# Score products over 128 rows instead of 128 and then 64, with keys padded by zeros

## The chip, the cores and the metric

The kernel runs on one core of one Trainium2 chip. The metric is the device time of one execution in microseconds (us). Three executions of the kernel before took 2716.71 us in the median (2715.36 to 2717.19).

## The reference

The reference is a network of three blocks on 512 tokens of width 1024, with a second stream of 256 context tokens in the last two. All is in 32-bit floats. The part that matters here is attention: four kinds of it, each of heads of 64 features.

```python
# first block: three dilated bands, joined over one row of weights
logits = jnp.einsum('bhrnqd,bhrnkd->bhrnqk', qb, kb) * Dh ** -0.5 + bias[None, :, None, None]
p = jnp.exp(logits - m[..., None])
num = jnp.einsum('bhrnqk,bhrnkd->bhrnqd', p, vb)
```

The second block has a differential attention (4 heads, each the difference of two maps of 64 features, over all 768 keys for the 512 tokens and over the 256 context keys for the context) and a neighbourhood attention (8 heads, blocks of 128 queries that see 256 keys around them and the 256 context keys). The third has a grouped attention (8 query heads, 2 key heads, 512 queries by 768 keys). All else in the network (a gated delta rule beside the dilated attention, projections, feed-forward layers, a long convolution) is not touched.

## The kernel before, in words

**Split products.** Each product of 32-bit operands is made of products of two rounded parts: a = hi + lo, both in the format that TensorE takes at full rate. A projection takes three matmuls (hi hi, hi lo, lo hi, lines 323 to 325), a score two, as follows.

**Scores.** A tile of 128 rows holds the features of two heads, 64 rows each. Since one head fills only half of the 128 rows of TensorE's array, the other half carries the small parts. `stacked` (line 1544) makes from keys [128, n] a tile [128, 2, n]: in `[:, e]` the 64 rows of head e hold its high parts and the other 64 rows its low parts. It takes one copy on ACT (line 1548) and two subtractions on POOL over 64 rows (line 1550). `doubled` (line 1553) makes from 128 queries the high parts of head e on both halves of the rows, and, in `lo`, the low parts of both heads, each on its own rows (ACT line 1557, POOL lines 1558 and 1560). `scores` (line 1563) then issues two matmuls for each up to 512 keys (line 1571): the first over 128 rows, q hi times k hi plus q hi times k lo; the second over the 64 rows of head e only, q lo times k hi, added in PSUM. In the grouped attention the roles are turned: the queries are stacked, and the keys, which stand twice in the rows, are split into `kl` and `kh` by `halves`; its second matmul also takes 64 rows.

**Stages.** The work on an item (a tile of 128 queries and a head, or both maps in the differential attention) is a list of steps, load, score, turn (transpose the weights, line 435, and copy them out of PSUM, lines 1581 and 1583), apply (times the values), end. `skewing` (line 1524) lets step i of an item come with step i - 1 of the next; a load stands two steps ahead of its score. Between score and turn `exp_rows` (line 892) takes the row maximum on DVE (line 903, or 899 with a bias) and the exponential on ACT (line 904 or 901). The scores have two PSUM rooms.

- The dilated attention of the first block (`dilated`, line 910) runs beside the recurrence of the delta rule, some of its steps with every round of it. Its keys are stacked in a room of the raw weights (`wraw`).
- In the second block `diff_attention` (line 1713) and `neighbourhood` (line 1586) are one list of items. Their keys are stacked in a tile `ks` with two rooms, once for each of four heads (pairs of maps) and of four pairs of heads. The value products are on line 1758 (over 128 columns), and on lines 1643 and 1702 (over 64 columns).
- In the third block `pair_attention` (line 1669) does the grouped attention, 32 items. Its value products are on line 1702 (64 columns).

**Rooms for weights.** `wchunk` (line 306) loads 512 KB of weights into one of two raw rooms, copies the high parts to one of three rooms `whi` on ACT (line 311), and subtracts the low parts into one of three rooms `wlo` on POOL (line 312). The last projection ahead of the attention in the second block is that of `vb`; the next weights after it are those of the out-projection.

**Order.** The instructions of each engine run in the order in which a planner has put them when the program is built (`schedule_with_timeline_sim=True`). It keeps what depends on what, and otherwise takes the work in the program's order as soon as its own estimate of times says it can start; later weights are split ahead of earlier attention where rooms are free.

## Time and profile before

| | |
|---|---|
| median of three timed executions | 2716.71 us |
| the profiled execution, its span from the first to the last instruction | 2708.6 us |
| TensorE (PE) busy | 2582.3 us, 95% |
| TensorE's weight loads (PEld) busy | 2093.1 us, 77% |
| VectorE (DVE) busy | 1636.8 us, 60% |
| GpSimd (POOL) busy | 1187.8 us, 44% |
| ScalarE (ACT) busy | 981.1 us, 36% |
| chain that ended last, by engine | PE 76%, DVE 15%, DMA 3%, issue 2% |
| mean granted clock of TensorE | 0.972 |

For the profiled execution the trace gives the span; the timed executions, which start and end outside of it, are 6.8 to 8.6 us longer. Busy shares are over the whole span. Matmuls are pipelined: a new one starts before the one ahead has ended, so the spacing from start to start says what one costs in a stream, and the duration does not. The chain of waits follows the work back from the last instruction to what released it; its shares say where time would be won if a piece became shorter and nothing else came in its place.

### The profile page before, as it was taken

To read this page: it belongs to the slowest core of one execution; us is meant where nothing else is said; L and a number is where in the kernel's file an instruction comes from. 1 tells how busy PE (TensorE), PEld (TensorE's weight loads), DVE (VectorE), ACT (ScalarE), POOL (GpSimd) and SP (SyncE) were. 2 spreads that over 40 slices of the span, in tenths; PEclk is the share of its full clock that TensorE was granted. 3 is DMA by queue.
4 is the path that set the end of the run, shared out by engine and by line. 5 is a ranking of instruction groups with operands and counts; after the bars stand their busy time and mean duration, and the time that the engine had idled before them with its cause. 6 is when DMAs were issued, how large, how long until landed. Compare 5 with 4: busy or idle time off the path is not lost.

```text
span 2708.6 us, 35291 instructions
## 1 busy us (share of the span) xinstructions
PE 2582.3 (95%) x13312; PEld 2093.1 (77%) x13312; DVE 1636.8 (60%) x2896; ACT 981.1 (36%) x1727; POOL 1187.8 (44%) x827
## 2 busy tenths in 40 slices
PE   8878999999999978999999999999999999999999
PEld 6667776788888757666788888888878778788887
DVE  6987546634434798776547677767576445634333
ACT  4514434322224323375524222122244543333232
POOL 3346525555556434676514232323245215444443
PEclk9989989999999989898999999999999999999999
DMA  5251112232333244301022343424242003233333
GB/s 198 81 182 46 31 55 94 86 100 88 99 102 124 98 155 139 110 17 28 28 102 86 111 134 111 138 93 149 76 136 75 20 24 124 87 95 96 104 95 94
DMA packets 103453, 257.94 MB, mean 95 GB/s; under 512 B 11745, under 2 KB 20065, under 8 KB 102900
## 3 DMA queue, kind: packets, MB, share of 16 engines
q1 hardware_dynamic: 102708, 254.64, 29.2%
q8 instruction: 105, 1.72, 0.3%
q10 hardware_dynamic: 576, 1.05, 0.1%
q14 instruction: 64, 0.52, 0.1%
HBM read 246.06 MB, written 14.83 MB: 96 GB/s over the span
## 4 chain that ended last, share of the span: by engine, by line
PE 76%; DVE 15%; DMA 3%; issue 2%; POOL 1%; ACT 1%; SPq 0%; POOLq 0%; DVEq 0%; ACTq 0%
PE ps_mm L323 13%; PE ps_mm L325 13%; PE ps_mm L324 13%; PE ps_s L1571 5%; PE ps_mx L324 3%; PE ps_mx L325 3%; PE ps_mx L323 3%; PE ps_m L324 3%; PE ps_m L323 3%; PE ps_m L325 3%; PE ps_t L435 3%; DVE ada_j L1093 2%; PE ps_pv L1702 2%; DVE ada_w L1093 2%; DMA ada_w<-in_w_ada 2%
## 5 line engine op out<-in xcount | busy, mean ns | idle before, releaser
L312 POOL TENSOR_TENSOR wlo<-wraw,whi 128x1024 fp32r<-128x1024 f32 (+2 forms) x344 | 776.3, 2260 | 1116.5 <-ACT whi L311 1034.8
L311 ACT ACTIVATE whi<-wraw 128x1024 fp32r<-128x1024 f32 (+2 forms) x345 | 336.8, 978 | 968.4 <-PE ps_mm L324 479.1
L323 PE MATMUL ps_mm<-h,whi 128*128 128x512 f32 (+1 forms) x1496 | 540.7, 363 | 11.8 <-ACT whi L311 7.3
L325 PE MATMUL ps_mm<-h,wlo 128*128 128x512 f32 (+1 forms) x1496 | 539.5, 362 | 2.3 <-POOL wlo L312 2.3
L324 PE MATMUL ps_mm<-h,whi 128*128 128x512 f32 (+1 forms) x1496 | 539.4, 362 | 1.2 <-DVE h L1145 1.0
L323 PEld LDWEIGHTS ps_mm<-h,whi 128*128 128x128 f32 x1496 | 282.4, 189 | 57.1 <-ACT whi L311 7.3
L325 PEld LDWEIGHTS ps_mm<-h,wlo 128*128 128x128 f32 x1496 | 282.0, 189 | 48.9 <-POOL wlo L312 2.9
L324 PEld LDWEIGHTS ps_mm<-h,whi 128*128 128x128 f32 x1496 | 282.2, 189 | 47.4 <-issue 1.7
L1093 DVE CUSTOM_DVE_ANT_0 ada_j<-ada_w,ada_c 128x512 f32<-128x512 f32 x192 | 195.9, 1020 | 14.7 <-DMA ada_w<-in_w_ada 14.2
L1093 DVE CUSTOM_DVE_ANT_0 ada_w<-ada_w,ada_c 128x512 f32<-128x512 f32 x192 | 186.2, 970 | 4.0
L325 PE MATMUL ps_mm<-fa,wlo 128*128 128x512 f32 (+1 forms) x528 | 186.3, 356 | 1.4 <-POOL wlo L312 1.4
L324 PE MATMUL ps_mm<-fa,whi 128*128 128x512 f32 (+1 forms) x528 | 187.6, 356 | 0.0
L323 PE MATMUL ps_mm<-fa,whi 128*128 128x512 f32 (+1 forms) x528 | 185.7, 356 | 0.0
L1270 DVE SCALAR_TENSOR_TENSOR cb<-ps_mm,small,cb 128x511 f32<-128x511 f32 (+1 forms) x66 | 43.6, 660 | 188.8 <-ACT cb L1268 188.8
L1218 DVE SCALAR_TENSOR_TENSOR x<-ps_mm,mod,x 128x512 f32<-128x512 f32 x80 | 59.4, 748 | 138.4 <-PE ps_mm L325 131.4
L903 DVE TENSOR_REDUCE nm<-ps_s 128x1 f32<-128x768 f32 (+1 forms) x96 | 74.6, 777 | 63.6 <-PE ps_s L1571 63.0
L325 PEld LDWEIGHTS ps_mm<-fa,wlo 128*128 128x128 f32 x528 | 99.0, 188 | 18.0 <-POOL wlo L312 2.0
L324 PEld LDWEIGHTS ps_mm<-fa,whi 128*128 128x128 f32 x528 | 99.2, 188 | 16.0
L323 PEld LDWEIGHTS ps_mm<-fa,whi 128*128 128x128 f32 x528 | 98.9, 188 | 16.4 <-ACT whi L311 0.3
L324 PE MATMUL ps_mx<-h,whi 128*128 128x512 f32 x216 | 86.1, 399 | 3.0 <-DVE h L1005 3.0
L323 PE MATMUL ps_mx<-h,whi 128*128 128x512 f32 x216 | 85.8, 399 | 0.5 <-ACT whi L311 0.5
L325 PE MATMUL ps_mx<-h,wlo 128*128 128x512 f32 x216 | 85.7, 397 | 0.0
(490 smaller groups left out, 5234.5 us busy)
## 6 DMA issues: line engine op xcount, KB each, us to landing
ada_w<-in_w_ada SPq DMA_DIRECT2D x192, 256.0 KB
wraw<-in_w_up SPq DMA_DIRECT2D x88, 512.0 KB
wraw<-in_w_d SPq DMA_DIRECT2D x48, 384.0 KB
wraw<-in_w_d SPq DMA_DIRECT2D x53, 320.0 KB
wraw<-in_we_in SPq DMA_DIRECT2D x24, 512.0 KB
wraw<-in_w_g SPq DMA_DIRECT2D x22, 512.0 KB
wraw<-in_w_u SPq DMA_DIRECT2D x22, 512.0 KB
wraw<-in_we_out SPq DMA_DIRECT2D x13, 512.0 KB
```

Of the source, the lines that this page charges most:

```text
L311: self.S.activation(hi[:, :n], raw[:, :n], AF.Copy)
L312: (eng or self.G).tensor_tensor(out=lo[:, :n], in0=raw[:, :n], in1=hi.bitcast(F32)[:, :n], op=ALU.subtract)
L323: mm(ps, lhi, rhi, start=start, stop=False)
L324: mm(ps, lhi, rlo, start=False, stop=False)
L325: mm(ps, llo, rhi, start=False, stop=stop)
L435: last = self.PE.transpose(ps[:, j * P:(j + 1) * P], src[:, j * P:(j + 1) * P], self.ident)
L903: V.tensor_reduce(out=m, in_=src, op=ALU.max, axis=AX.X, negate=True)
L1093: V.tensor_tensor_reduce(out=(junk, w)[s], in0=w, in1=c[:, s, i * T:i * T + T], scale=0.5, scalar=0.0, op0=ALU.mult, op1=ALU.add, accum_ou ...
L1218: V.scalar_tensor_tensor(out=xs[s][:, m], in0=p[:, :w], scalar=mod[:, gate * 8 + m, s:s + 1], in1=xs[s][:, m], op0=ALU.mult, op1=ALU.add)
L1270: V.scalar_tensor_tensor(out=cb[:, t0 + 1:t1], in0=pg[s][:, :w_ - 1], scalar=fw[0], in1=cb[:, t0 + 1:t1], op0=ALU.mult, op1=ALU.add)
L1571: self.PE.matmul(p[:, c0:min(n, c0 + 512)], q[i], k[i][:, c], start=i == 0, stop=i == 1)
L1702: PE.matmul(st["v"][hs, t * P:(t + 1) * P], vals(e, kt), st["t", t, e][:, kt * P:(kt + 1) * P], start=kt == 0, stop=kt == nk - 1)
```

## The change

The second matmul of a score takes all 128 rows as well. Its query operand is `lo` as it stands, with the low parts of both heads. Its key operand is a new tile `kz`: in `[:, e]` the 64 rows of head e hold its high parts, and the other rows are zero. Two such tiles are set to zero once on POOL at the start of the dilated attention (512 columns) and of the attention of the second block (768 columns), and the own rows are filled for each pair of heads by two copies of 64 rows on ACT. In the second block they take the place of the two rooms of `ks`; the stacked keys of the two heads go to a room of `whi` and a room of `wlo`, and so the copy over both becomes one for each. In the dilated attention they stay in the raw room, also with a copy for each. In the grouped attention no tile is added: the second matmul takes the stacked queries and the low parts of the keys on all 128 rows, which adds the product of the low parts. (The diff also takes comments and descriptions out of the file.)

```diff
+    def zeroed(self, pool, n, nm="kz"):
+        tiles = [pool.tile([P, 2, n], F32R, name=f"{nm}{i}", bufs=1) for i in range(2)]
+        for z in tiles:
+            for e, (own, other) in enumerate(HALVES):
+                self.G.memset(z.bitcast(F32)[other, e], 0.0)
+        return tiles
-    def stacked(self, at, src, nm, bufs=2, st=None):
-        if st is None:
-            st = at.tile([P, 2, src.shape[-1]], F32R, name=nm + "s", bufs=bufs)
-        self.S.activation(st, self.midb(src, 2), AF.Copy)
+    def stacked(self, at, src, nm, bufs=2, kz=None, st=None):
+        n = src.shape[-1]
+        if kz is None:
+            room = at.tile([P, 2, n], F32R, name=nm + "s", bufs=bufs)
+            st = [room[:, e] for e in range(2)]
+            self.S.activation(room, self.midb(src, 2), AF.Copy)
+        else:
+            st = st or [self.wh.tile([P, CH], F32R, name=w)[:, :n] for w in ("whi", "wlo")]
+            for a in st:
+                self.S.activation(a, src, AF.Copy)
         for e, (own, other) in enumerate(HALVES):
-            self.G.tensor_tensor(out=st[other, e], in0=src[own], in1=st.bitcast(F32)[own, e], op=ALU.subtract)
-        return st
+            self.G.tensor_tensor(out=st[e][other], in0=src[own], in1=st[e].bitcast(F32)[own], op=ALU.subtract)
+        if kz is None:
+            return st
+        for e, (own, other) in enumerate(HALVES):
+            self.S.activation(kz[own, e], src[own], AF.Copy)
+        return st, [kz[:, e] for e in range(2)]
...
+        kzs = self.zeroed(da, T)
...
-                                st["k", pair] = self.stacked(da, self.dk[:, pair], "k",
-                                                       st=room.rearrange("p (e t) -> p e t", e=2))
+                                st["k", pair] = self.stacked(da, self.dk[:, pair], "k", kz=kzs[pair % 2],
+                                                             st=[room[:, :T], room[:, T:]])
...
-                        (q, lo), k = st["q", pair, qt], st["k", pair]
-                        self.scores(p[:, :n], (q[:, e], lo[hs]), (k[:, e, :n], k[hs, e, :n]))
+                        (q, lo), (k, kz) = st["q", pair, qt], st["k", pair]
+                        self.scores(p[:, :n], (q[:, e], lo), (k[e][:, :n], kz[e][:, :n]))
...
+                kzs = self.zeroed(at, TC)
...
-                            st["k", pair] = self.stacked(at, ka[:, pair], "k")
+                            st["k", pair] = self.stacked(at, ka[:, pair], "k", kz=kzs[pair % 2])
...
-                        q = q[:, e], lo[hs]
-                        k = st["k", pair][:, e], st["k", pair][hs, e]
+                        q = q[:, e], lo
+                        k = [a[e] for a in st["k", pair]]
...
-                    q = (q[:, e], q[hs, e]) if form == "stacked" else (q[0][:, e], q[1][hs])
+                    q = (q[e], q[e]) if form == "stacked" else (q[0][:, e], q[1])
...
-                        st["k", hd] = self.stacked(at, qkb[hd // 2][:, 1, hd % 2], "k")
+                        st["k", hd] = self.stacked(at, qkb[hd // 2][:, 1, hd % 2], "k", kz=kzs[hd % 2])
...
-                        (q, lo), k, hs = st["q", hd, t], st["k", hd], HALVES[e][0]
-                        self.scores(p, (q[:, e], lo[hs]), (k[:, e, k0:], k[hs, e, k0:]))
+                        (q, lo), (k, kz) = st["q", hd, t], st["k", hd]
+                        self.scores(p, (q[:, e], lo), (k[e][:, k0:], kz[e][:, k0:]))
...
-                            return self.kd2[0], self.kd2[1][HALVES[e][0]]
+                            return self.kd2
```

## Rows read from the trace of the kernel before

**Rows 1.** Stretches: length, busy us (and count) of PE, PEld, DVE, ACT, POOL, clock, DMA.
```profile
205.00:380.00 175.00, 166.39 (x1299) 134.50 (x1298) 105.27 (x268) 82.81 (x185) 96.30 (x122) 0.98 0.11 32
1137.00:1257.00 120.00, 111.72 (x507) 76.56 (x505) 81.87 (x204) 80.56 (x218) 82.59 (x112) 0.87 0.09 25
1257.00:1371.00 114.00, 110.59 (x722) 82.22 (x723) 68.55 (x189) 56.97 (x158) 56.87 (x92) 0.97 0.14 44
2106.00:2235.00 129.00, 129.00 (x769) 91.79 (x768) 55.46 (x108) 62.82 (x121) 26.02 (x38) 1.00 0.05 17
```

**Rows 2.** Chain of waits, shares by line: 205:380, 1137:1257, 1257:1371, 2106:2235.
```profile
by line: PE ps_p L760 11.4%; PE ps_p L754 11.4%; PE ps_pv L954 10.8%; PE ps_p L435 10.8%; PE ps_a L1571 8.1%; PE ps_a L435 6.3%; DVE ada_j L1093 6.0%; DVE ada_w L1093 4.3%; PE ps_a L431 2.5%; PE ps_p L720 2.5%; PE ps_p L776 2.4%; PE ps_o L8
...
by line: PE ps_s L1571 43.4%; PE ps_pv L1758 22.2%; PE ps_t L435 12.0%; POOL E L1747 3.9%; issue 3.8%; DVE nm L903 2.8%; POOL E L1748 1.9%; ACT E L904 1.8%; DVE E L1743 1.3%; DVE er L1741 1.2%; POOL ql L1558 1.1%; ACT PT L1581 0.9%; DVE PT 
...
by line: PE ps_s L1571 39.2%; PE ps_pv L1643 25.9%; PE ps_t L435 20.5%; PE ps_t L431 4.4%; PE ps_pv L1702 4.0%; PE ps_pv L1758 1.3%; DVE da_o L1768 0.9%; DVE da_o L1769 0.8%; DVE nm L903 0.7%; DVE h L319 0.6%; ACT h L318 0.5%; DVE rsq_a L30
...
by line: PE ps_s L1571 33.1%; PE ps_pv L1702 31.7%; PE ps_t L435 20.8%; PE ps_t L323 3.1%; PE ps_t L324 2.8%; PE ps_t L325 2.8%; PE ps_t L431 2.2%; PE ps_mm L323 1.2%; PE ps_mm L324 1.2%; PE ps_mm L325 1.2%
```

**Rows 3.** Timeline of PE, grouped attention: start us, us, engine, line, operation, tiles, rows*columns, shape.
```profile
2136.22 0.48 PE L1571 MATMUL ps_s<-kh,qs 128*128 128x512 f32 x1
2136.63 0.49 PE L1571 MATMUL ps_s<-kl,qs 64*128 64x512 f32 x1
2137.05 0.38 PE L1571 MATMUL ps_s<-kh,qs 128*128 128x256 f32 x1
...
2137.68 0.50 PE L1571 MATMUL ps_s<-kh,qs 128*128 128x512 f32 x1
...
2141.99 0.47 PE L1571 MATMUL ps_s<-kh,qs 128*128 128x512 f32 x1
```

**Rows 4.** Timeline of PEld, a plain stream and the grouped attention; idle before in brackets.
```profile
601.68 0.19 PEld L324 LDWEIGHTS ps_mx<-h,whi 128*128 128x128 f32 x1
...
2136.63 0.18 PEld L1571 LDWEIGHTS ps_s<-kl,qs 64*128 64x128 f32 x1 [0.24 <-issue]
```

**Rows 5.** Timeline of PE, plain streams of 512 and of 256 columns.
```profile
599.63 0.39 PE L323 MATMUL ps_mx<-h,whi 128*128 128x512 f32 x1
...
601.90 0.39 PE L324 MATMUL ps_mx<-h,whi 128*128 128x512 f32 x1
...
1599.16 0.28 PE L323 MATMUL ps_mm<-fa,whi 128*128 128x256 f32 x1
...
1599.96 0.28 PE L324 MATMUL ps_mm<-fa,whi 128*128 128x256 f32 x1
```

**Rows 6.** Timeline of PE, grouped attention: the last score matmul and the value products.
```profile
2138.86 0.38 PE L1571 MATMUL ps_s<-kl,qs 64*128 64x256 f32 x1
2139.17 1.09 PE L1702 MATMUL ps_pv<-PT,gv 128*64 128x128 f32 x8
```

**Rows 7.** Timeline of DVE and ACT, grouped attention: row maximum and exponential.
```profile
2137.78 0.96 DVE L903 TENSOR_REDUCE nm<-ps_s 128x1 f32<-128x768 f32 x1 [0.85 <-PE ps_s L1571]
...
2138.78 0.90 ACT L904 ACTIVATE E<-ps_s,nm 128x768 f32<-128x768 f32 x1 [0.52 <-DVE nm L903]
```

**Rows 8.** Copies and splits by line: duration ns min/median/max, first and last start, forms.
```profile
L1548 ACT ACTIVATE ks<-qkb x4: 1472/1478/1487, 1114.2 to 1190.0; 128x1536 fp32r<-128x1536 f32 x4
...
L1422 ACT ACTIVATE qkb<-ps_t x12: 582/598/602, 1042.8 to 1112.7; 128x512 f32<-128x512 f32 x12
...
L311 ACT ACTIVATE whi<-wraw x345: 257/1060/1140, 6.2 to 2695.0; 128x1024 fp32r<-128x1024 f32 x121, 128x640 fp32r<-128x640 f32 x27, 128x768 fp32r<-128x768 f32 x24, 128x64 fp32r<-128x64 f32 x1
L312 POOL TENSOR_TENSOR wlo<-wraw,whi x344: 318/2394/3714, 14.6 to 2695.8; 128x1024 fp32r<-128x1024 f32 x122, 128x640 fp32r<-128x640 f32 x26, 128x768 fp32r<-128x768 f32 x24
```

**Rows 9.** Groups of POOL by line: busy us, mean ns, idle before.
```profile
L678 POOL MEMSET Pw<- 128x512 f32 x2 | 1.0, 540 | 10.8 <-DVE ada_p L1093 10.8
```

**Rows 10.** A weight chunk's copy on ACT; line 1571 in the second block, first and last.
```profile
1129.50 1.06 ACT L311 ACTIVATE whi<-wraw 128x1024 fp32r<-128x1024 f32 x1 [7.23 <-PE ps_m L325]
...
L1571 PE MATMUL ps_s<-ks,qd x160: 355/385/775, 1137.5 to 1365.1; 128*128 128x256 f32 x128, 128*128 128x512 f32 x32
```

More of the change, by code (lines that the diff above doesn't have):

```diff
@@ L1492, in even_mixer @@
                 at = self.pool(ats, "at", 2, "right")
+                kzs = self.zeroed(at, TC)
+                consts += kzs,
                 values = lambda half: em.tile([P, 2, 2, TC], F32, name=f"vw{half}", tag=f"qkb{half}")
-                self.skewed(self.diff_attention(at, ps, qkb, vb, lam, oms)
+                self.skewed(self.diff_attention(at, ps, qkb, vb, lam, oms, kzs)
                             + self.neighbourhood(consts, values, at, ps, qa, ka, vc, vad, oms))
@@ L1587, in neighbourhood @@
         V, S, G, PE, Q, A = self.V, self.S, self.G, self.PE, self.Q, self.A
-        mask, biases = consts
+        mask, biases, kzs = consts
         nb = len(biases)
@@ L1623, in score @@
                             st["r", pair] = at.tile([P, 4, 2], F32, name="rr")
-                        hs = slice(64 * e, 64 * e + 64)
                         p = self.s_bank(ps)
                         q, lo = st["q", pair, b]
-                        q = q[:, e], lo[hs]
-                        k = st["k", pair][:, e], st["k", pair][hs, e]
+                        q = q[:, e], lo
+                        k = [a[e] for a in st["k", pair]]
                         win = [a[:, 0:T].rearrange("p (r c) -> p r c", c=64)[:, :, w0s[b]:w0s[b] + 32] for a in k]
@@ L1653, in neighbourhood @@
                 at, ps, qa[:, pair, T:TC], "doubled",
-                lambda e, pair=pair: (st["k", pair][:, e, T:], st["k", pair][HALVES[e][0], e, T:]), 2, 2,
+                lambda e, pair=pair: [a[e][:, T:] for a in st["k", pair]], 2, 2,
                 lambda e, kt, pair=pair: vc[:, kt, (2 * pair + e) * 64:(2 * pair + e) * 64 + 64], oms[1][:, :, pair, :])
@@ L1684, in load, with score @@
                     st["q", t] = getattr(self, form)(at, qT[:, t * P:(t + 1) * P], "q", 3)
-                def score(t=t, e=e, hs=hs):
+                def score(t=t, e=e):
                     if t == 0 and e == 0:
@@ L1711, in pair_attention, with diff_attention @@
         return items
-    def diff_attention(self, at, ps, qkb, vb, lam, oms):
+    def diff_attention(self, at, ps, qkb, vb, lam, oms, kzs):
         V, S, G, PE, Q, A = self.V, self.S, self.G, self.PE, self.Q, self.A
```

## The prediction

> **What bounds the kernel now.** I read the page's table of engines first: TensorE is busy for nearly the whole span and no other engine comes near it. A busy TensorE says little here, since the ends of matmuls are modelled, so I went on to the stages in which line 1571, the score matmul, runs. The table by stretches [rows 1] shows four of them: the dilated attention beside the recurrence (205 to 380 us), the differential attention (1137 to 1257), the neighbourhood attention (1257 to 1371) and the grouped attention (2106 to 2235). The reader is to see that the other engines stand at half to two thirds of a stretch, and that only the differential stretch has three engines above 80 of 120 us. Then the chain of waits, cut to the same stretches [rows 2]: the largest part of the chain in three of them is line 1571, with 43.4%, 39.2% and 33.1%; beside the recurrence it has 8.1%. In time that is 0.434 x 120 = 52.1, 0.392 x 114 = 44.7, 0.331 x 129 = 42.7 and 0.081 x 175 = 14.2 us, 154 us in all. That is the time the change can work on.
>
> What this time is made of is seen in the timeline of TensorE [rows 3]. A score product of 768 keys is four matmuls: 512 columns over 128 rows, 512 over 64, 256 over 128, 256 over 64. From start to start the first takes 0.41 us, the second 0.42, the two of 256 together 0.63, so 0.315 each. A plain stream that stays at 128 rows does the same columns far faster [rows 5]: ten spacings of 512 columns in 2.27 us, 0.227 each, and seven of 256 in 0.80, 0.114 each. The columns are the same, all at the full granted clock; the rest, about 0.19 to 0.2 us, is paid at each change between 128 and 64 rows. The weight loads show it too [rows 4]: in the plain stream the load (601.68) runs under the matmul ahead of its own (601.90, [rows 5]), while at the change the load starts only with its own matmul and TensorE's loader has idled 0.24 us ahead of it.
>
> **The change part by part.**
> *The second matmul over 128 rows.* No matmul is added or taken away and no column. The changes 128 to 64 within a product go, and 64 to 128 behind it, unless a value product on 64 columns comes next: there the spacing is also 0.31 [rows 6], and that change of shape remains. Two items of the grouped stage have 2.95 us of scores (2136.22 to 2139.17, [rows 3, 6]); without changes it is 2 x (2 x 0.227 + 2 x 0.114) = 1.36, plus 0.2 for the one that remains: 1.57, saving 1.38 or 47%. Two neighbourhood items have eight of 256, 8 x 0.315 = 2.52, and then 0.91 to 1.11: I take 56%. The differential stage mixes both sizes and part of it is at the lower clock (0.87 on the mean, [rows 1]), where the columns themselves take longer: 50%. For the dilated one with its sizes from 128 to 512 I take 45%. On the chain that is at most 20 + 25 + 26 + 6 = 77 us. The other end is nothing, if what is late next is right behind.
>
> *What is late next.* Grouped stage: the weights of an item need its row maximum and the exponential. From the end of the scores (2137.68) they are there at 2138.78 + 0.90 = 2139.68 [rows 7], 2.0 us later. Today TensorE covers that with the next item's scores and a value product. After the change the first item's scores end at 0.68, its weights are ready at about 2.7, and TensorE has done the other scores and the eight value products (1.09, [rows 6]) at about 2.4: it waits 0.3 us. Two items go from 5.77 (2136.22 to 2141.99, [rows 3]) to 5.77 - 1.38 + 0.3 = 4.7; sixteen such pairs give 17 us, and I take 16 for the edges. The neighbourhood stage has more slack (DVE 69, ACT 57, POOL 57 of 114 us, [rows 1]) but the same kind of chain: two thirds of 25, 17. In the differential stage DVE, ACT and POOL have 82, 81 and 83 us of 120; with all 26 us gone, 94, they would have to be busy nearly 90% while waiting for each other at every item. I take 11, with ends 26 and 0. Beside the recurrence, whose chain is mostly its own products, 2 of the 6.
>
> *The split of the keys.* Per pair of heads ACT did one copy of 128x1536 in 1.48 us [rows 8]. Now it does two of 128x768 and two of 64x768. No row has this size; between 0.60 for 512 columns and 1.06 for 1024 I put 0.83, an estimate. Four are 3.3, so 1.84 more for each of eight pairs, 14.7 us, and in the dilated stage, by 4 x 0.60 - 1.06, 1.34 for each of four, 5.4: 20 us of ACT in all. POOL's two subtractions stay. I put the 20 us at nothing on the path in the neighbourhood and the dilated stage, since ACT has 57 and 92 us free there [rows 1] and a pair is loaded two steps ahead; the differential stage's 7.4 is part of why I take only 11. If the cover is gone it is the whole 20, since exponentials queue behind the copies on ACT and TensorE waits for them. In the grouped stage nothing is added.
>
> *The zeros.* Four POOL memsets in either stage. 128x512 took 0.54 [rows 9]; by that, 2.2 us in the dilated stage and, scaled to 768 columns, 3.2 in the even layer. The latter lie ahead of 1137, when the last projection still has TensorE: nothing. The former may stand in the recurrence's way: 0 to 2.2, in the 2 us above.
>
> *The room for split weights.* The stacked keys now take turns with the weight chunks in three rooms. The first pairs wait for the last projection's chunks: a weight chunk's copy that took such a room waited until 1129.50 [rows 10]. The second pair can thus have its copies at about 1130, and POOL's subtractions have 7 us behind them until scores begin at 1137.5: nothing. At the end, the third chunk of the out-projection gets its room only behind the last scores (1365, [rows 10]) and then needs 1.06 on ACT and 2.39 on POOL [rows 8]; transposes, value products and the end of the heads still run then. 0 to 3.5 us; I take 0, as its products come third.
>
> **Sum.** 16 + 17 + 11 + 2 = 46 us off the profiled execution's span, 2708.6 to 2663. The timed runs lie around it with a median of 2716.71, 8.1 above the span; I keep that distance: 2671 us. Taken by itself this forecast has 2655 to 2687.
>
> **Rivals.**
> *The other engines take it back (2695).* If the chains of maximum, exponential and transpose close up sooner, half the gain stays: 8 + 9 + 4 + 1 = 22. For it: DVE, ACT and POOL in the differential stage. Against: the other two have room.
> *All of it (2640).* The 77 us come out whole. For it: the chain in the grouped stage has TensorE nearly alone [rows 2], and the order of instructions is planned anew. Against: the 2.0 us from scores to weights.
> *Slower: ACT's copies on the path (2717 to 2737, say 2727).* Place: ACT's queue at each load of a pair, 3.3 us in one piece in front of the exponentials, with two score banks. Price: 20 us. It decides once the drains give back under 20 us; half of that given back is plus 10. For it: in the differential stretch ACT has 81 of 120 us. Against: it waits for the scores there, and far more time lies on line 1571 than 20 us.
> *The change of rows is not what costs (2716).* If the load of weights can't run under a matmul on the same rows, a product costs load plus stream: 0.19 + 0.227 = 0.41 for 512 columns, as now, and 0.30 for 256, as now within 0.02. Nothing is won, and the copies cost little. The plain stream speaks against it: the load of 0.19 at 601.68 is over before its matmul starts at 601.90, and lies wholly under the matmul ahead, on the same 128 rows [rows 4, 5].
> This is the rule of the Trainium skill's page "TensorE: Matmul & The Clock Gate" (Part 3, The mechanism): a weight load overlaps with running matmuls only when it goes to another row group. By it the old mix of 64 and 128 rows would be no worse than the new form and the time would stay at 2716; by the rows the spacing falls to 0.227. Here the rows decide.
>
> **How the numbers follow.** The forecast has 0.52, the half gain 0.22, the whole gain 0.12, slower 0.08, no effect 0.06. A measurement of this kernel can tell about 0.2% (5.4 us) from no change. So faster 0.86, same 0.06, slower 0.08. The range goes from 2640, where the whole gain ends, to 2702, which takes in the half gain and some loss at the seams (the end of the attention, a new order of work); outside are the slower case, the case without effect and a little on either side.
>
> **What would show it.** Right: score matmuls of 512 columns about 0.23 apart and those of 256 about 0.115, but 0.31 still ahead of value products; the weight loads of the second matmuls under the first; the grouped stretch down from 129 to about 113 us, the neighbourhood from 114 to 97, the differential from 120 to about 109; longer waits of TensorE for ACT and DVE. Wrong: spacings unchanged (no effect of rows); spacings short but stretches as long as before, with TensorE waiting for the exponential behind four key copies in a row (the slower rival); stretches shorter but a new wait of the out-projection for its third chunk.

## The result: 2652.9 us, a ratio of 0.977

The changed kernel took 2652.91 us in the median of four executions (2645.98 to 2653.69), the kernel before 2716.95 on the same chip (2715.36 to 2719.39): a ratio of 0.9767, with a 95% interval of 0.9749 to 0.9785, or 64 us less. The forecast was 2671, 46 us less, with a range of 2640 to 2702; the time lies inside the range, but 2 us below the 2655 to 2687 that the forecast had claimed for itself, and nearer to the rival of 2640. The profiled executions are 57.5 us apart in span (2708.6 and 2651.1): the one lies 8.4 us below its median, the other 1.8, so 6.5 of the 64 us are not in the stages below. The changed kernel's profiled execution took 2.0 us more than its own span (2653.09 and 2651.1), so most of the 8.4, which had been read as time outside of the span, means that the profiled execution of the kernel before was a quick one.

The stages of all kernels of this study, worked out from the traces as the time between two landmarks. Behind the stroke stands how much of the stage had TensorE at the lower granted clock, 1.2 GHz. Each row is a single profiled execution.

| us / of it at 1.2 GHz | start | dilated | block 1 | projection | differential | neighbourhood | feed-forward | projection 3 | grouped | rest |
|---|---|---|---|---|---|---|---|---|---|---|
| before | 204.1/27 | 204.1/23 | 566.8/35 | 162.5/17 | 126.0/31 | 111.2/7 | 657.9/0 | 78.3/0 | 132.6/0 | 460.5/10 |
| the change | 201.2/17 | 199.1/19 | 567.0/36 | 162.4/24 | 118.7/31 | 88.9/7 | 660.0/3 | 78.3/0 | 111.0/0 | 459.6/7 |
| e1, grouped only | 203.2/24 | 203.2/16 | 564.6/28 | 162.5/24 | 127.7/34 | 111.3/7 | 661.1/3 | 78.3/0 | 111.3/0 | 459.4/7 |
| e2, second block only | 203.8/23 | 203.9/23 | 566.9/36 | 163.2/21 | 114.0/14 | 89.3/7 | 660.1/3 | 78.3/0 | 132.6/0 | 460.7/10 |
| e3, dilated only | 203.5/24 | 202.3/33 | 567.3/36 | 162.5/17 | 143.0/68 | 109.3/3 | 659.5/3 | 78.2/0 | 132.6/0 | 460.6/10 |
| e12, e3 with fillers | 204.4/26 | 195.9/18 | 565.2/31 | 160.5/21 | 145.4/34 | 109.0/7 | 660.0/7 | 78.2/0 | 132.6/0 | 460.3/10 |
| e4, same rows together | 203.5/27 | 203.3/16 | 564.6/28 | 162.3/21 | 113.0/24 | 111.7/7 | 659.2/0 | 78.3/0 | 120.8/0 | 459.5/7 |
| e5, copies twice | 199.7/21 | 210.7/53 | 567.1/35 | 162.6/24 | 115.8/21 | 88.0/7 | 660.7/7 | 78.2/0 | 111.1/0 | 460.9/10 |
| e7, no POOL in the difference | 203.2/24 | 202.4/33 | 567.2/36 | 160.6/21 | 109.3/17 | 88.2/7 | 659.0/3 | 78.2/0 | 111.3/0 | 460.7/10 |
| e8, values on 128 columns | 202.9/24 | 202.5/32 | 567.4/36 | 162.7/17 | 114.5/17 | 89.3/7 | 662.6/10 | 78.3/0 | 105.8/3 | 460.8/10 |
| e9, fillers | 200.1/21 | 200.5/23 | 564.3/32 | 162.8/17 | 114.3/14 | 88.7/7 | 657.1/0 | 78.3/0 | 111.5/0 | 460.5/10 |
| e10, e7 and e8 | 203.4/27 | 198.5/22 | 564.7/26 | 160.4/14 | 109.1/17 | 88.2/7 | 659.1/3 | 78.3/0 | 101.9/0 | 460.3/10 |
| e11, e10 and fillers | 203.4/24 | 197.7/18 | 565.0/26 | 162.7/17 | 105.7/0 | 89.4/7 | 658.6/3 | 78.2/0 | 107.0/3 | 459.8/10 |

(Landmarks, each the start of a matmul: a late projection product ahead of the dilated attention; the first out-projection product of block 1 behind it; a late product of the second block's norm; the first score; the last value product of the differential attention; the first out-projection product; a late feed-forward product; the first grouped score; the first product of the long convolution; the last product.)

Between before and the change the dilated stage has 5.0 us less, the differential 7.3, the neighbourhood 22.3, the grouped 21.6, together 56.2 of the 57.8 in the table. How far a stage moves without any edit can be read from the differential column: the changed kernel, e2 and e8 have the same order of instructions there on TensorE, VectorE, ScalarE and GpSimd, and took 118.7, 114.0 and 114.5 us, with 31, 14 and 17 us at 1.2 GHz. A microsecond at the lower clock cost some 0.3 us in this order, in which TensorE also waits for other engines.

The first view to look at is the timeline of TensorE in the grouped attention, which answers to [rows 3] and [rows 6].

```profile
2101.92 0.48 PE L1593 MATMUL ps_s<-kh,qs 128*128 128x512 f32 x1
2102.24 0.39 PE L1593 MATMUL ps_s<-kl,qs 128*128 128x512 f32 x1
2102.47 0.28 PE L1593 MATMUL ps_s<-kh,qs 128*128 128x256 f32 x1
2102.59 0.28 PE L1593 MATMUL ps_s<-kl,qs 128*128 128x256 f32 x1
2102.71 0.38 PE L435 MATMUL ps_t<-ident,E 128*128 128x128 f32 x2
2103.02 1.52 PE L1723 MATMUL ps_pv<-PT,gv 128*64 128x128 f32 x12
...
2104.88 0.48 PE L1593 MATMUL ps_s<-kh,qs 128*128 128x512 f32 x1
...
2108.81 0.28 PE L1593 MATMUL ps_s<-kl,qs 128*128 128x256 f32 x1
2109.02 1.09 PE L1723 MATMUL ps_pv<-PT,gv 128*64 128x128 f32 x8
2110.04 0.44 PE L435 MATMUL ps_t<-ident,E 128*128 128x128 f32 x2
```

From start to start the four score matmuls take 0.32, 0.23, 0.12 and 0.12 us, 0.79 in all, where they took 1.46. Only the first, behind a transpose, is longer than in a plain stream. Where value products on 64 columns come next (2108.81 to 2109.02), the last one takes 0.21, not the 0.31 of [rows 6].

The weight loads answer to [rows 4]. The load of the second matmul starts at 2102.01 and its matmul at 2102.24, so it lies under the matmul ahead.

```profile
2102.01 0.19 PEld L1593 LDWEIGHTS ps_s<-kl,qs 128*128 128x128 f32 x1
```

The table by stretches of the changed kernel, as in [rows 1], with the four stages' own bounds: dilated, differential, neighbourhood, grouped.

```profile
201.00:400.00 199.00, 181.69 (x1416) 148.25 (x1414) 119.81 (x311) 88.00 (x197) 99.69 (x123) 0.95 0.16 47
1130.00:1248.00 118.00, 90.54 (x543) 78.64 (x542) 92.08 (x217) 91.76 (x246) 91.95 (x122) 0.87 0.08 21
1248.00:1337.00 89.00, 82.10 (x715) 70.86 (x714) 63.37 (x178) 57.41 (x156) 52.22 (x84) 0.96 0.15 47
2076.00:2187.00 111.00, 110.89 (x817) 91.94 (x816) 54.33 (x109) 61.99 (x122) 20.98 (x30) 1.00 0.06 20
```

And the chain of waits in the last three of them, as in [rows 2].

```profile
by line: PE ps_pv L1779 11.8%; PE ps_s L1593 11.7%; POOL E L1768 10.4%; PE ps_t L435 7.9%; issue 7.8%; DVE E L1764 6.2%; POOL E L1769 6.0%; DVE nm L903 5.7%; DVE er L1762 5.0%; POOL qd L1582 4.3%; ACT E L904 3.0%; POOL ql L1580 3.0%; DVE rs
...
by line: PE ps_pv L1664 30.3%; PE ps_t L435 24.1%; PE ps_s L1593 19.9%; PE ps_pv L1723 6.6%; PE ps_t L431 6.3%; DVE rsq_i L301 2.2%; issue 1.2%; DVE da_o L1790 1.1%; DVE da_o L1789 1.1%; DVE PT L1605 0.8%; DVE h L319 0.8%; DVE nm L903 0.7%;
...
by line: PE ps_pv L1723 41.7%; PE ps_t L435 23.5%; PE ps_s L1593 19.2%; PE ps_t L323 3.5%; PE ps_t L431 3.4%; PE ps_t L324 3.3%; PE ps_t L325 3.1%; ACT whi L311 1.0%; ACT PT L1603 0.5%; ACT hy_x L1984 0.5%; PE ps_mm L323 0.4%; issue 0.2%; A
```

The reader is to see two things. In the neighbourhood and the grouped stage TensorE still has nearly the whole chain, and is busy for 82 of 89 and 111 of 111 us: nothing has come in the place of the score matmuls, and they fell from 39.2% and 33.1% to 20% and 19%. In the differential stage they fell from 43.4% to 11.7%, the chain is now spread over POOL, DVE and ACT, and these three are busy for 92 of 118 us each while TensorE has 91.

How much of the work went, and how much came back as waiting, is told by the same view between the landmarks of the table: differential and neighbourhood, first of the kernel before, then of the changed one.

```profile
1137.50:1263.51 126.01, 117.73 (x542) 81.11 (x541) 88.17 (x217) 85.51 (x234) 88.18 (x119) 0.88 0.10 27
1263.51:1374.68 111.17, 107.25 (x718) 79.64 (x716) 63.63 (x177) 54.27 (x148) 51.28 (x85) 0.97 0.13 41
```

```profile
1129.62:1248.29 118.67, 91.21 (x547) 79.25 (x546) 92.37 (x217) 92.40 (x248) 92.16 (x123) 0.87 0.08 21
1248.29:1337.19 88.90, 82.00 (x713) 70.59 (x711) 63.08 (x178) 57.12 (x154) 52.01 (x83) 0.96 0.16 48
```

In the differential stage TensorE's busy time fell by 26.5 us and its idle time grew from 8.3 to 27.5. In the neighbourhood stage they are 25.3 us less and 3.9 to 6.9.

The copies, zeros and rooms. Columns are duration in ns (least, median, most), the first and the last start.

```profile
L1552 POOL MEMSET kz<- x8: 517/627/736, 21.9 to 1111.6; 64x512 f32 x4, 64x768 f32 x4
L1572 ACT ACTIVATE kz<-dk x8: 620/628/633, 181.0 to 280.2; 64x512 fp32r<-64x512 f32 x8
L1572 ACT ACTIVATE kz<-qkb x8: 829/836/845, 1106.3 to 1182.1; 64x768 fp32r<-64x768 f32 x8
```

The copy of 768 columns took 0.84 us where 0.83 had been put. The zeros of the dilated stage were set at 22 us, far ahead of it. The third chunk of the out-projection came late, as forecast: its copy behind the last scores, its subtraction over before its product.

```profile
1329.58 1.06 ACT L311 ACTIVATE whi<-wraw 128x1024 fp32r<-128x1024 f32 x1 [0.64 <-PE ps_s L1593]
...
1331.30 2.36 POOL L312 TENSOR_TENSOR wlo<-wraw,whi 128x1024 fp32r<-128x1024 f32 x1 [5.48 <-PE ps_s L1593]
...
1337.19 0.50 PE L323 MATMUL ps_mm<-h,whi 128*128 128x512 f32 x1
```

### The profile page after: what moved, and what is told of

It is laid out like the page before. It is cut to its first block, busy times and chain, and to the rows that moved or that the text cites. A ratio compares the mean times of both kernels' runs of the same rounds, so it can differ in the third digit from the quotient of the medians.

```text
span 2651.1 us, 35356 instructions
## 1 busy us (share of the span) xinstructions
PE 2500.5 (94%) x13312; PEld 2078.7 (78%) x13312; DVE 1631.5 (62%) x2896; ACT 996.5 (38%) x1763; POOL 1192.6 (45%) x835
## 4 chain that ended last, share of the span: by engine, by line
PE 73%; DVE 17%; DMA 3%; issue 2%; POOL 2%; ACT 2%; SPq 0%; POOLq 0%; DVEq 0%; ACTq 0%
PE ps_mm L323 14%; PE ps_mm L325 14%; PE ps_mm L324 14%; PE ps_mx L324 3%; PE ps_mx L325 3%; PE ps_mx L323 3%; PE ps_m L324 3%; PE ps_m L323 3%; PE ps_m L325 3%; PE ps_t L435 2%; DVE ada_w L1094 2%; DVE ada_j L1094 2%; PE ps_s L1593 2%; PE ps_pv L1723 2%; DMA ada_w<-in_w_ada 2%
## 5 line engine op out<-in xcount | busy, mean ns | idle before, releaser
L323 PE MATMUL ps_mm<-h,whi 128*128 128x512 f32 (+1 forms) x1496 | 540.5, 363 | 11.7 <-ACT whi L311 7.2
L1094 DVE CUSTOM_DVE_ANT_0 ada_j<-ada_w,ada_c 128x512 f32<-128x512 f32 x192 | 184.3, 960 | 13.1 <-DMA ada_w<-in_w_ada 12.6
L435 PE MATMUL ps_t<-ident,E 128*128 128x128 f32 x464 | 79.9, 292 | 20.4 <-POOL E L1769 13.6
```

Of the source, the lines that this page charges most:

```text
L323: mm(ps, lhi, rhi, start=start, stop=False)
L435: last = self.PE.transpose(ps[:, j * P:(j + 1) * P], src[:, j * P:(j + 1) * P], self.ident)
L1094: V.tensor_tensor_reduce(out=(junk, w)[s], in0=w, in1=c[:, s, i * T:i * T + T], scale=0.5, scalar=0.0, op0=ALU.mult, op1=ALU.add, accum_ou ...
```

## The experiments

**One stage alone (e1, e2, e3).** Each is the kernel before with the change in one of the three places; e1 is

```diff
-                    q = (q[:, e], q[hs, e]) if form == "stacked" else (q[0][:, e], q[1][hs])
+                    q = (q[:, e], q[:, e]) if form == "stacked" else (q[0][:, e], q[1][hs])
...
-                            return self.kd2[0], self.kd2[1][HALVES[e][0]]
+                            return self.kd2
```

> The kernel before, with the second matmul over 128 rows in the grouped attention alone; no copy, no memset and no room is added there, and the other stages stay. If each change of rows costs about 0.2 us, the whole loss of that stage comes back as in the changed kernel: 21 us, about 2696 us, with the grouped stretch shorter by about 20 us and all others as before. If TensorE only waits for the weights of an item instead (maximum and exponential are 2.0 us behind the scores), 16 us or less, 2701. If the changed kernel's gain there came from a new order of work that the earlier stages brought about, little: 2710 or more.

Measured: 2691.87 us against 2712.98, ratio 0.9914 (0.9899 to 0.9929), 21 us less. The grouped stage went from 132.6 to 111.3 us; of the others none moved by more than 3.2. No work was added here, so the 21 us are the second matmul's rows alone. TensorE's order in this stage is the one of the kernel before, with two items' scores in a row, and the two items of [rows 3] can be found again:

```profile
2134.12 0.47 PE L1571 MATMUL ps_s<-kh,qs 128*128 128x512 f32 x1
...
2136.09 0.90 ACT L904 ACTIVATE E<-ps_s,nm 128x768 f32<-128x768 f32 x1 [0.52 <-DVE nm L903]
...
2136.70 0.88 PE L435 MATMUL ps_t<-ident,E 128*128 128x128 f32 x6
...
2138.50 0.48 PE L1571 MATMUL ps_s<-kh,qs 128*128 128x512 f32 x1
```

They take 4.38 us in place of 5.77, 1.39 less, which is what the spacings alone give. The wait of 0.3 us that the forecast had put here did not come: the transposes behind the value products start at 2136.70, while the exponential of the first of the two items runs until 2136.99, so they begin with the weights of an earlier item.

> The change in the second block's attention alone (differential and neighbourhood): padded keys, four more copies per pair on ACT, keys in the rooms of split weights. In the changed kernel the second block's attention gave back 30 us and 1.6 us went again right behind it. If the parts add up: 28 us, 2689 us. If ACT's copies cost on the path, the split by stage shows it in the differential stretch: 113 us there against 120 before.

Measured: 2682.63, ratio 0.9884 (0.9869 to 0.9898), 30 us less. The neighbourhood stage lost 21.9 us, the differential one 12.0, with half the time at 1.2 GHz that it has in the kernel before and in the changed one. Its order of instructions there is the changed kernel's, so the 4.7 us between these two are not the edit. The 1.6 us behind the attention that I had laid to the third chunk's room are in e1 too (feed-forward 661.1), where no room is shared; they are not the rooms.

> The change in the dilated attention alone. The changed kernel was 7.7 us ahead at the end of that stage, where 2 were forecast. If the parts add up: 8 us, 2709 us. If the 7.7 are a new order of the recurrence's work beside it rather than the score products, the order and the gain may not come again: 2714 to 2718.

Measured: 2721.24, ratio 1.0031 (1.0019 to 1.0042): 8 us slower, which no theory had. The dilated stage itself lost 1.8 us, with 9 us more at 1.2 GHz than before. What got longer is the differential attention, whose program is that of before: 143 us against 126. Its instructions stood in another order (the planner starts from other times when the stage ahead has changed), and TensorE's clock was at the lower level for 68 us of it:

```profile
1136.00:1279.00 143.00, 134.21 (x546) 92.52 (x545) 92.80 (x220) 85.52 (x236) 88.95 (x121) 0.76 0.08 23
```

A mean granted clock of 0.76 over 143 us is 68 us at half speed. Half of the 37 us more at 1.2 GHz is 19, and the stage is 17 longer. It is not waiting: between the landmarks TensorE sat idle for 8.8 us, before for 8.3, over the same number of matmuls and nearly as many changes of shape (180 and 176). Nor is it one odd execution: the mean granted clock over the whole kernel was 0.962 to 0.969 in all twelve, and 0.968 to 0.974 in the seventeen of the kernel before. The three medians of e1, e2 and e3 add to 43 us less, not 64; these 17 us are most of what is missing.

**Fillers (e12).** The kernel of e3, with matmuls whose result nobody reads, to keep TensorE busy in that stage.

```diff
+                    idle = st["k", hd][0]
+                    for _ in range(4):
+                        PE.matmul(pv[:, P:], idle[:, :P], idle[:, :T - P], start=True, stop=True)
```

> The kernel with the change in the dilated attention alone, which was 8 us slower than before, with four matmuls of 384 columns behind each item of the differential attention, into columns that nobody reads. In that kernel the differential attention, whose program is that of before, stood in another order and took 143 us with 68 of them at 1.2 GHz (126 with 31 before). If the lower clock is what made it slower: with the fillers the low stretch falls to 15 to 30 us and the attention to 112 to 122, about 2695 to 2703 us in all. If the order itself is worse (waits of TensorE for other engines): the 16 us of fillers come on top or fill waits only, 2718 to 2735.

Measured: 2717.6, ratio 1.0013 (1.0000 to 1.0026), which overlaps that of e3. The time at 1.2 GHz fell as the first theory said, to 34 us from 68, but the stage stayed at 145 us:

```profile
1126.00:1271.00 145.00, 138.33 (x647) 99.80 (x646) 97.63 (x224) 86.99 (x239) 85.04 (x122) 0.88 0.09 25
```

So neither expectation came as written: 17 us given back by the clock, and the fillers, which cost 16 us by themselves, lay on the path, since with the changes of rows TensorE has few waits there to fill. Against the kernel before, with nearly the same time at 1.2 GHz (34 and 31 us), the stage is 19 us longer, and 16 of these are the fillers: the order itself costs little, and the clock explains the length of e3. Why the clock fell for so long in that order is not shown. It does not go with TensorE's waits: e3 has 8.8 us of them with 68 at 1.2 GHz, e2 28.9 with 14. The fillers also came with a new order of their own, so that they were what raised the clock is not shown either.

**Is it the change, or the 64 rows? (e4)**

```diff
-        for c0 in range(0, n, 512):
-            c = slice(c0, min(n, c0 + 512)) if n > 512 else slice(None)
-            for i in range(2):
+        for i in range(2):
+            for c0 in range(0, n, 512):
+                c = slice(c0, min(n, c0 + 512)) if n > 512 else slice(None)
```

> The kernel before, 64-row matmuls and all, but where a score has 768 keys the two matmuls over 128 rows come first and the two over 64 rows behind them, so that two changes of rows are left of four. It tells the cost of a change from a cost of 64 rows as such. If the change costs: the spacing from a 512-column matmul over 64 rows to the next over 64 rows falls to about 0.23 us, the grouped stretch loses 32 x 2 x 0.19 = 12 us, the differential one a few, the neighbourhood one nothing (its products have 256 columns): about 2702 us. If 64 rows are slow in themselves: spacings of 0.42 and 0.31 stay behind the 64-row matmuls, and at most half of that gain comes.

Measured: 2685.2, ratio 0.9891 (0.9876 to 0.9906), 28 us less. The grouped stage lost 11.8 us, as worked out for two changes less of four; the neighbourhood one nothing (its products have 256 columns); the differential one 13.0, more than the few expected. That had been counted too low: this stage also has 32 score products of 768 keys (4 heads, 4 tiles, 2 maps), so 12 us as well; it had 7 us less at 1.2 GHz besides. In the timeline each row now holds the two matmuls of one form, 512 and 256 columns:

```profile
2103.06 0.59 PE L1571 MATMUL ps_s<-kh,qs 128*128 128x512 f32 x2
2103.58 0.61 PE L1571 MATMUL ps_s<-kl,qs 64*128 64x512 f32 x2
2104.12 0.62 PE L1571 MATMUL ps_s<-kh,qs 128*128 128x512 f32 x2
2104.66 0.61 PE L1571 MATMUL ps_s<-kl,qs 64*128 64x512 f32 x2
2105.21 1.52 PE L1702 MATMUL ps_pv<-PT,gv 128*64 128x128 f32 x12
```

Over 64 rows a pair takes 0.54 to 0.55 us, as over 128 rows: the columns (0.227 + 0.114 = 0.34) and one change of 0.2. Within a pair the spacing did not fall to the 0.23 expected: the trace has 0.335 over 64 rows and 0.338 over 128, since about half of the 0.2 falls on the matmul ahead of a change and half on the first one behind it. Matmuls over 64 rows are not slow, as far as these pairs show; the change is. A count agrees. From the first to the last score of the grouped stage the kernel before has 182 changes of shape between one matmul and the next, e4 122, e1 68, and this takes 118.2, 106.5 and 97.2 us: 0.17 to 0.2 us for each change that went.

In the differential stage grouping alone came to 113.0 us, and no kernel with the padding that leaves POOL's two instructions in place was shorter (114.0 to 118.7). There the runs show no gain of the padding over the turned loop.

**ACT's copies (e5).**

```diff
             self.S.activation(kz[own, e], src[own], AF.Copy)
+            self.S.activation(kz[own, e], src[own], AF.Copy)
```

> The changed kernel with each of the copies into kz done twice on ACT: 16 more of 0.84 us in the second block and 8 of 0.63 in the dilated attention, 18 us of ACT in all, as much again as the change itself added. If the copies lie beside other work, as forecast: within 4 us of the changed kernel, 2653 to 2657. If ACT's queue at the loads sets the pace (the slower rival): all of it, 2671, and so the change itself had paid as much.

Measured: 2661.45, ratio 0.9794 (0.9781 to 0.9808), 8.5 us above the changed kernel, between the two expectations; the intervals of the two kernels overlap. Its stages, dilated, differential, neighbourhood:

```profile
200.00:410.00 210.00, 195.28 (x1413) 157.04 (x1412) 118.50 (x313) 90.76 (x201) 101.38 (x123) 0.87 0.14 44
1140.00:1256.00 116.00, 90.43 (x567) 78.40 (x565) 95.96 (x230) 100.47 (x263) 94.46 (x126) 0.91 0.09 25
1256.00:1344.00 88.00, 81.21 (x692) 69.89 (x692) 58.88 (x166) 57.20 (x150) 49.71 (x80) 0.96 0.18 57
```

In the neighbourhood stage (88.0 against 88.9) the copies cost nothing. In the differential stage ACT is busy for 9 us more and the stage is 2.9 shorter, with 10 us less at 1.2 GHz. The three kernels of one order (114.0, 114.5 and 118.7 us for 14, 17 and 31 at 1.2 GHz) would have some 115.5 for e5's 21, and e5 has 115.8: no cost of the copies can be told there. The dilated stage is 11.6 longer, with 53 us at the lower clock against 19. Half of these 34 us would be 17, so the clock alone can account for it, but the copies and the clock are not separated. The slower rival, which needs the copies on the path in the second block, is out.

**What is late next in the differential stage (e7).** One DVE instruction over 768 columns in place of one over 512 and two on POOL.

```diff
-                    c = slice(0, min(n, T))
+                    c = slice(0, n)
...
-                    if n > T:
-                        c = slice(T, n)
-                        G.tensor_scalar(out=e2[:, c], in0=e2[:, c], scalar1=r2, scalar2=None, op0=ALU.mult)
-                        G.tensor_tensor(out=e1[:, c], in0=e1[:, c], in1=e2[:, c], op=ALU.add)
```

> The changed kernel with the last 256 columns of the difference of the two maps on DVE, with the other 512, in place of two POOL instructions (1.3 and 0.8 us, 16 items, 34 us of POOL; DVE gets some 5 us more). In the changed kernel the chain through the differential stretch has POOL's two instructions with 17%, and TensorE waits 14 us for them. If they are what comes late next: the stretch of 113 us loses 8 to 12, about 2643 us. If DVE (75 us of 113) or the lower clock holds it: no gain, 2650 to 2658.

Measured: 2643.8, ratio 0.9734 (0.9719 to 0.9750), 9 us below the changed kernel, whose interval it just touches. The stage went from 118.7 to 109.3, though with 14 us less at 1.2 GHz. Next to e8, which has the changed kernel's order there and as much time at 1.2 GHz (17 us), it is 5 us shorter (114.5); so 5 of the 9 are the edit, and the rest came with the clock. TensorE's longest waits in the stage, first of the changed kernel, then of e7 (engine and line, for whom, us in total, times, longest):

```profile
PE ps_t L435 <- POOL E L1769: 13.6, 13, 1.9
PE ps_t L435 <- DVE E L1764: 5.4, 6, 2.3
```

```profile
PE ps_s L1593 <- ACT E L904: 7.0, 4, 3.2
PE ps_s L1593 <- POOL qd L1582: 4.3, 5, 1.3
```

The 13.6 us of waiting for POOL's line 1769 went with that line; 7.0 for ACT stand first now. POOL was late next, and right behind it comes ACT, busy for 92.8 of 110 us:

```profile
1133.00:1243.00 110.00, 86.96 (x560) 75.83 (x560) 88.68 (x226) 92.77 (x254) 63.78 (x93) 0.92 0.09 24
```

**The change of columns that is left (e8).** In the grouped attention a head's values stand beside zeros, the two heads of a pair in either half, and twelve products go into one sum on all columns.

```diff
+                    vz = at.tile([P, 2, 2, 6, P], F32, name="gvz", bufs=1)
+                    for e in range(2):
+                        G.memset(vz[:, :, e, :, HALVES[1 - e][0]], 0.0)
+                        for u in range(2):
+                            G.tensor_copy(vz[:, u, e, :, HALVES[e][0]], v[:, :, u * 64:u * 64 + 64])
...
-                            lambda e, kt, pr=pr: v[:, kt, (pr // 2) * 64:(pr // 2) * 64 + 64],
+                            lambda e, kt, pr=pr: vz[:, pr // 2, e, kt],
...
-                                  start=kt == 0, stop=kt == nk - 1)
+                                  start=kt == 0 and not (wide and e), stop=kt == nk - 1 and not (wide and not e))
```

> The changed kernel with the value products of the grouped attention on all 128 columns, the values of a head beside zeros and both heads of a pair into one sum; so no change of shape is left between scores, transposes and value products there. Same number of matmuls; four copies and two memsets on POOL more, once. If a change of columns costs what a change of rows does (0.31 against 0.11 behind 256 columns, 0.20 against 0.11 behind 128): 32 items with about 0.2 on the way in and 0.1 on the way out, 8 to 10 us, 2644 us. If TensorE has come to wait for ACT and DVE there: nothing.

Measured: 2648.9, ratio 0.9755 (0.9740 to 0.9770); its interval overlaps that of the changed kernel. The stage itself went from 111.0 to 105.8 us, 5 of the 8 to 10 expected, with 3 us at the lower clock, which it had not had, and a wait of 2.2 us of TensorE for an exponential on ACT.

```profile
2106.65 0.27 PE L1593 MATMUL ps_s<-kl,qs 128*128 128x256 f32 x1
2106.76 1.05 PE L1723 MATMUL ps_pv<-PT,gvz 128*128 128x128 f32 x8
2107.65 0.82 PE L435 MATMUL ps_t<-ident,E 128*128 128x128 f32 x6
2108.30 0.61 PE L1723 MATMUL ps_pv<-PT,gvz 128*128 128x128 f32 x4
```

From the last score matmul to the value products it is 0.11 us, where the timeline of the changed kernel above has 0.21 (2108.81 to 2109.02), and eight value products up to the next transpose take 0.89, where it has 1.02 (2109.02 to 2110.04). The trace of single matmuls divides this. At either end of a run on 64 columns the matmul ahead takes 0.09 to 0.10 more, and the first one behind 0.05 more (0.160 to 0.166 to its next, where the others have 0.109). A change of columns thus costs 0.15 us each way.

**Fillers in the changed kernel (e9).** The same edit as in e12, with `kzs[hd % 2][:, 0]` as operand.

> The changed kernel with four matmuls of 384 columns behind the value products of each item of the differential attention, into columns that nobody reads; 96 of about 0.165 us, 16 us of TensorE at the full clock. In that stretch the granted clock was 1.2 GHz for 31 of 113 us in the changed kernel, 14 in the run with the second block's change alone and 68 in the run with the dilated attention's alone, and the stretch was about half of that longer each time. If more matmuls keep the clock up and lie in TensorE's waits: a stretch of 100 to 108 us, 2640 to 2648. If the clock falls as before: up to 16 us more, 2655 to 2669.

Measured: 2643.87, ratio 0.9735 (0.9722 to 0.9748), 9 us below the changed kernel. The whole time lies where the first theory had it; the stage, 4.4 us shorter with 14 us at 1.2 GHz in place of 31, misses its 100 to 108. Nor does it prove the theory: e2, with the changed kernel's order and no filler, has the same 14 us and 114.0. What can be said is that 96 more matmuls cost the stage nothing that can be told, since they lie in TensorE's waits (14.4 us idle, 28.9 in e2). The other 4.6 are scattered over stages that the edit doesn't touch.

```profile
1128.00:1242.00 114.00, 99.62 (x652) 89.05 (x651) 96.92 (x227) 90.80 (x254) 91.14 (x127) 0.94 0.09 24
```

**The edits together (e10, e11).** e10 is the changed kernel with the edits of e7 and e8; e11 has the fillers too.

> The changed kernel with both edits that gave something: the difference of the maps on DVE alone, and the grouped attention's value products on 128 columns. They lie in different stages; by the stages (9 us in the differential one, 5 in the grouped one) 2639 us, if the clock does not fall elsewhere; 2632 to 2646.

Measured: 2629.44, ratio 0.9693 (0.9674 to 0.9713), 83 us below before and, by the two ratios, 20 below the changed kernel: the fastest of the study, and below what was expected. The grouped stage came to 101.9 us, so the change of columns is worth the 9 us worked out where TensorE never waits and the clock stays up.

```profile
1127.00:1236.00 109.00, 85.93 (x554) 74.96 (x553) 87.96 (x223) 92.00 (x252) 63.42 (x92) 0.92 0.09 24
2062.00:2163.00 101.00, 101.00 (x810) 95.08 (x809) 54.11 (x108) 61.67 (x122) 23.95 (x34) 1.00 0.10 33
```

> As the kernel with both edits, and the fillers of the differential attention too. If the clock in that stretch still has 17 us at the lower level, the fillers give back up to 4 of them net of their own time; with POOL off the path TensorE waits less there, and they can cost more than before: 2632 to 2645.

Measured: 2634.73, ratio 0.9712 (0.9693 to 0.9731). The differential stage has no time at 1.2 GHz any more and is 3.4 us shorter than in e10, but the grouped stage, with the same program, came out in 107.0 and took that back. There TensorE waited once for ACT, 3.3 us, and then had 3.4 us at 1.2 GHz; with half of the latter that is 5.0 of the 5.1. In e8 it is 2.2 and half of 3.4, 3.9 of 3.9. One wait, in another order of the same work, takes back half of that edit. The two kernels' intervals overlap.

## Why the prediction was right, and where its sizes were off

*What bounds the kernel.* Right. The time lay in the spacing of score matmuls, and e4 shows that it is the change of rows that costs, 0.2 us each, and not the 64 rows. The size was low: 2652.9 lies between the forecast and the rival by which all of it comes (2640). In the grouped and the neighbourhood stage that rival's terms came (20 and 25 us; 21.6 and 22.3 found), in the differential one the forecast's.

*The spacings.* Right for 0.23 and 0.12 in the place of 0.42 and 0.315. Ahead of value products 0.31 had been left as it was, and 0.21 came: that spacing had two changes in it, of rows and of columns, and only the columns' stayed. The rival by which the weight load could not run under a matmul on the same rows is out: the load at 2102.01 runs under the matmul ahead. So the sentence of the Trainium skill that was weighed against the rows ("TensorE: Matmul & The Clock Gate", Part 3) does not hold here: loads of weights overlap with running matmuls on the same 128 rows, and it is at a change of rows that they did not [rows 4]. What the rows show agrees with another of its pages, "TensorEngine Tiling (Array Packing)" (Key Properties), by which a change of the tiling mode drains TensorE. That these 0.2 us are such a drain no run shows; they are what the change costs here.

*Grouped stage, 16 us forecast, 21.6 found.* This is the step that was off. The chain's share gave 20; I took off a wait of 0.3 us for each two items, because the weights come 2.0 us behind the scores. The 0.1 us of the row above adds 1.6 for sixteen pairs, and the wait, 4.8 for sixteen pairs, did not come: 16 + 4.8 + 1.6 = 22.4, near what was found. TensorE is busy for 110.9 of 111 us, and in the chain ACT and DVE are hardly there. The new order of work is not the reason, since e1 kept the old one and its stage took 111.3 us with one wait of 0.4. The error was to let TensorE need an item's weights right behind the eight value products: what stands there are transposes of an earlier item.

*Neighbourhood stage, 17 forecast, 22.3 found.* The same error by analogy: a third was taken off the 25 for chains that hardly closed up. TensorE's busy time fell by 25.3 us, and 3.0 came back as waits. The copies on ACT cost nothing there (e5).

*Differential stage, 11 forecast, 7.3 found.* The reason was right: the other three engines stand in the way, POOL first (e7), then ACT. TensorE's busy time fell by 26.5 us, the 26 of the bound, and 19.2 came back as waits where 15 had been taken off. The difference of 3.7 is no more than the same order of instructions moves by itself: e2 and e8 lost 12.0 and 11.5. What I had not priced is the clock, 14 us at 1.2 GHz in the one and 31 in the changed kernel; that 11 comes so near to 12.0 and 11.5 is in part luck, since it was a choice between 0 and 26.

*Dilated stage, 2 forecast, 5.0 found; 1.8 in e3.* The part differs with the time at 1.2 GHz, 19 us in the one and 33 in the other. At 16 to 23 us of it the four kernels without the change there have 203.2 to 204.1 us and the five with it (the change, e9 to e12) 195.9 to 200.5. So the sign is shown, 3 to 8 us, and no single size.

*Zeros, rooms, copies: nothing on the path.* Right for the zeros (set at 22 us and ahead of the first scores) and for the rooms (the third chunk was ready 3.5 us ahead of 1337.19). For the copies right in the neighbourhood stage, nothing that can be told in the differential one, open in the dilated one. The slower rival fell. That one part of the change alone, e3, is slower by 8 us came by a way that was not among the rivals: a lower clock, along with a new order, in a later stage.

## What to carry to other kernels

In the two stages whose chain had TensorE nearly alone, the spacings came back almost whole (21.6 of 20 us, 22.3 of 25); take off waits where another engine already has a part in the chain, and then name which. Price a change of matmul shape by the spacing from start to start against a plain stream of the same columns, and group matmuls of one shape where padding costs too much: that alone gave 28 of the 64 us, for a loop turned round. A stage that no edit touches moved by 5 us at the same order, and by 17 us with a new one, so read every stage and its granted clock before a gain is laid to an edit.

## What the runs showed of the hardware

- A change between matmuls over 128 and over 64 rows costs 0.2 us at the full clock behind 256 or 512 columns, in both directions, half on the matmul ahead and half on the first behind (e4: 0.205 in place of 0.114, 0.335 in place of 0.227); one between 128 and 64 columns 0.15, also divided (0.10 and 0.05). Both at once cost no more: in e4, where the last score matmul stands behind another over 64 rows, it has 0.205 ahead of the value products and the first of these 0.160. The 0.31 of [rows 6] holds half of the change into the 64 rows as well. A pair of matmuls over 64 rows is as fast as one over 128.
- The granted clock of the differential stage stood at 1.2 GHz for 0 to 68 us of 106 to 145. One order of instructions had 14, 17 and 31 us of it in three kernels, and TensorE's waits do not tell how much it will be (8.8 us idle with 68, 28.9 with 14). With 96 matmuls without use there were 14 where there had been 31, 0 for 17 and 34 for 68, each time in another order; that they are the cause is not shown, as 14 came without them too. They cost nothing that can be told where TensorE waits, and their 16 us in e12, where it hardly does.
- Time at 1.2 GHz costs about half of itself where TensorE hardly waits (e3 against before: 17 us for 37), and less where it does (the change against e2: 4.7 us for 17).
- A copy on ACT takes as long over 64 rows as over 128: 0.84 us and 0.83 to 0.85 for 768 columns, 0.63 and 0.62 for 512 (the changed kernel).
